# Wider moving operands in a two-layer transformer step: paired high and low activations for the first FFN matrix, token-major gate and branch projections, bias vectors loaded first

## The chip, the core and the metric

The program runs on one core of a Trainium2 chip. Its matrix engine (PE) multiplies a stationary 128x128 tile with a moving operand of up to 512 columns; the vector engine (DVE) and the scalar engine (ACT) work on rows of 128 partitions; SP issues the transfers. The metric is the device time of one execution in microseconds (us). What counts as computed is the whole of the reference: both token groups through both layers, and the two context states.

## The reference, cut to what matters

256 tokens (128 context and 128 latent) of width 2048 go through two layers. The layers' weights are float32 and each is used once per layer.

```python
shift1, scale1, gate1, shift2, scale2, gate2 = _modulation(cvec, p['w_mod'], p['b_mod'])
h = _rmsnorm(x, p['g_pre_mix']) * (1 + scale1) + shift1
au, av, q, k, v, ga, gb = jnp.split(h @ p['w_in'], SPLITS, axis=-1)
ya = _spatial_gating(au, av, ...)
yb, extra = attend(_heads(q), _heads(k), _heads(v))
merged = sigmoid(ga) * (ya @ p['w_pa']) + sigmoid(gb) * (_merge_heads(yb) @ p['w_pb'])
x = x + gate1 * _rmsnorm(merged @ p['w_out'], p['g_post_mix'])
h = _rmsnorm(x, p['g_pre_ffn']) * (1 + scale2) + shift2
f = jnp.square(jax.nn.relu(h @ p['w_ff1'])) @ p['w_ff2']
x = x + gate2 * _rmsnorm(f, p['g_post_ffn'])
```

## The kernel before, in words

**Products.** Every float32 factor is split into a high part (rounded to the float32r format) and a low part (the rest), and a product is the sum of three: high by high, low by high, high by low. A *job* is one weight tile of 128x1024 numbers: a transfer into `raw`, a high part `wh` that ACT writes, a low part `wl` that DVE writes (`split`, L319), and its matmuls (`mm_half`, L327). There are four buffers of `wh` and of `wl`, six of `raw`. A job covers two slices of 128 along the contracted dimension and 512 output columns. Eight jobs make a *group* for a contraction of 2048 (four for 1024), summed in one of two PSUM tiles `mm` of 128x1024.

**Two forms.** In the feature-major form (L346 to L352) the weight is stationary in 128x128 pieces and the activations of all 256 tokens move: 24 matmuls of 256 columns a job. In the token-major form (L339 to L344) the activations of 128 tokens are stationary and 512 weight columns move: 12 matmuls of 512 columns. Before, only the projections av and v are token-major, 64 of the 928 jobs.

**Stages.** The order is mixing, FFN, mixing, FFN. A mixing stage has 208 jobs: the input projections av, au, q, k, v (two groups each), four gate groups alternating with four branch projections pa, four alternating with pb, and four groups of wo. `post_pb` (L616) multiplies the gate in, adds the pa branch and splits the result; wo needs it feature-major. An FFN stage has 256 jobs in four blocks; in each, four groups of the first matrix (ff1) and four of the second (ff2). After an ff1 group `post_ff1` (L696) runs relu, square and the high part on ACT, then the low part on DVE.

**Around the stages.** At a boundary the columns are normed and the input of the next stage is made in four parts c = 0 to 3 by `h_part` (L286): DVE scales, DVE and ACT modulate, ACT rounds the high part, DVE takes the low part. `H_STEPS` lets parts 0 to 2 be issued ahead of the stage's first job and part 3 behind its third. The modulation matrices are read in 512 KB tiles throughout; 248 of them are dot products on DVE (`mod_dot`, two instructions of 128x1024 each), laid between the jobs by a quota and a load estimate. Sgu and attention run as background generators, one step per job (`pump`).

**What sets the order.** The program writes out one list of items by hand. Before each item `advance` issues loads, and splits while fewer than four split jobs wait for PE; then the item's matmuls follow, then dot products, then the group's post step. Each engine runs its own instructions strictly in that order.

## Time and profile before

| What | Value |
|---|---|
| median time of 3 runs | 2898.01 us (2897.16 to 2898.41) |
| profiled execution, first to last instruction | 2896.6 us |
| PE busy, weight loads busy | 98%, 94% |
| DVE busy, ACT busy | 71%, 46% |
| DMA, mean | 247 GB/s |
| feature-major matmuls (256 columns) | 20736 |
| token-major matmuls (512 columns) | 768 |

The profile gives no time of the profiled execution beyond its span, which is 1.4 us under the median. Busy time of PE is modelled from pipelined instructions that overlap each other, so the pace of matmuls is read from their starts, not from their mean durations. The groups view lists instructions by line, engine, operation and tile with busy time, mean duration and the idle time before them with what ended it; L80 is the helper through which all DVE and ACT instructions pass.

### The profile page before, as it was taken

To read this page: it belongs to the slowest core of one execution; us is meant where nothing else is said; L and a number is where in the kernel's file an instruction comes from. 1 tells how busy PE (TensorE), PEld (TensorE's weight loads), DVE (VectorE), ACT (ScalarE), POOL (GpSimd) and SP (SyncE) were. 2 spreads that over 40 slices of the span, in tenths; PEclk is the share of its full clock that TensorE was granted. 3 is DMA by queue.
4 is the path that set the end of the run, shared out by engine and by line. 5 is a ranking of instruction groups with operands and counts; after the bars stand their busy time and mean duration, and the time that the engine had idled before them with its cause. 6 is when DMAs were issued, how large, how long until landed. Compare 5 with 4: busy or idle time off the path is not lost.

```text
span 2896.6 us, 54382 instructions
## 1 busy us (share of the span) xinstructions
PE 2837.1 (98%) x22792; PEld 2718.1 (94%) x22792; DVE 2069.7 (71%) x2585; ACT 1331.0 (46%) x1614; POOL 0.7 (0%) x6
## 2 busy tenths in 40 slices
PE   7999999999999999999999999999999999999997
PEld 5788899998999999999979989999979999999997
DVE  4665778888688898888667887777566565665445
ACT  4344454444544534434454445544554444353443
POOL 0000000000000000000000000000000000000000
PEclk9999999999999999999999999999999999999999
DMA  8978877789568888888677786677666666666553
GB/s 346 383 257 309 284 234 234 264 283 347 191 226 275 273 274 269 282 272 275 239 278 245 225 285 220 206 239 246 248 239 201 209 213 219 215 204 190 181 184 109
DMA packets 199062, 714.91 MB, mean 247 GB/s; under 512 B 22304, under 2 KB 24864, under 8 KB 198816
## 3 DMA queue, kind: packets, MB, share of 16 engines
q1 hardware_dynamic: 198816, 711.43, 72.3%
q8 instruction: 178, 2.92, 0.4%
q14 instruction: 68, 0.56, 0.0%
HBM read 705.04 MB, written 6.31 MB: 246 GB/s over the span
## 4 chain that ended last, share of the span: by engine, by line
PE 95%; DVE 3%; ACT 1%; DMA 1%; issue 0%; SPq 0%; ACTq 0%; DVEq 0%
PE mm L350 29%; PE mm L351 28%; PE mm L352 28%; PE mm L342 2%; PE mm L343 2%; PE mm L344 2%; DVE u L80 2%; PE aux L237 2%; PE aux L256 1%; ACT u L80 1%; DMA u<-wm 0%; DVE wl L80 0%; DMA bmod<-bmod 0%; PE aux L497 0%; PE aux L539 0%
## 5 line engine op out<-in xcount | busy, mean ns | idle before, releaser
L350 PE MATMUL mm<-u,wh 128*128 128x256 f32 x6912 | 1962.3, 284 | 0.0
L351 PE MATMUL mm<-u,wh 128*128 128x256 f32 x6912 | 1956.7, 283 | 4.6 <-DVE u L80 4.6
L352 PE MATMUL mm<-u,wl 128*128 128x256 f32 x6912 | 1955.7, 283 | 0.0
L80 DVE TENSOR_TENSOR wl<-raw,wh 128x1024 fp32r<-128x1024 f32 x928 | 1122.6, 1223 | 575.1 <-ACT wh L80 564.9
L80 ACT ACTIVATE wh<-raw 128x1024 fp32r<-128x1024 f32 x928 | 972.9, 1058 | 1184.3 <-PE mm L351 1061.7
L350 PEld LDWEIGHTS mm<-u,wh 128*128 128x128 f32 x6912 | 1326.4, 192 | 20.4 <-issue 14.1
L351 PEld LDWEIGHTS mm<-u,wh 128*128 128x128 f32 x6912 | 1326.6, 192 | 6.0 <-DVE u L80 5.7
L352 PEld LDWEIGHTS mm<-u,wl 128*128 128x128 f32 x6912 | 1326.6, 192 | 0.0
L80 DVE SCALAR_TENSOR_TENSOR mraw<-mraw,sbc 128x1024 f32<-128x1024 f32 x225 | 275.7, 1225 | 7.8
L80 DVE SCALAR_TENSOR_TENSOR junk<-mraw,sbc 128x1024 bf16<-128x1024 f32 x225 | 274.3, 1219 | 0.0
L80 ACT ACTIVATE u<-u 128x1024 f32<-128x1024 f32 (+4 forms) x141 | 130.1, 926 | 112.8 <-DVE u L80 106.8
L80 DVE TENSOR_TENSOR u<-u,u 128x1024 fp32r<-128x1024 f32 (+4 forms) x98 | 100.8, 1028 | 97.3 <-ACT u L80 96.2
L80 ACT ACTIVATE u<-mm 128x1024 f32<-128x1024 f32 (+1 forms) x95 | 86.7, 925 | 156.0 <-PE mm L352 139.8
L80 DVE TENSOR_TENSOR u<-u,mm 128x1024 f32<-128x1024 f32 (+1 forms) x54 | 63.6, 1180 | 64.5 <-PE mm L352 52.7
L342 PE MATMUL mm<-wh,u 128*128 128x512 f32 x256 | 102.6, 401 | 4.4 <-ACT u L80 4.4
L343 PE MATMUL mm<-wh,u 128*128 128x512 f32 x256 | 101.3, 396 | 3.1 <-DVE u L80 3.1
L344 PE MATMUL mm<-wl,u 128*128 128x512 f32 x256 | 100.5, 393 | 0.0
L342 PEld LDWEIGHTS mm<-wh,u 128*128 128x128 f32 x256 | 48.6, 190 | 22.0 <-ACT wh L80 6.7
L343 PEld LDWEIGHTS mm<-wh,u 128*128 128x128 f32 x256 | 48.6, 190 | 14.8 <-DVE u L80 5.4
L344 PEld LDWEIGHTS mm<-wl,u 128*128 128x128 f32 x256 | 48.5, 189 | 10.3
L237 PE MATMUL aux<-mraw,csw 128*32 128x512 f32 (+1 forms) x336 | 44.5, 590 | 12.0 <-DMA mraw<-wm 11.9
L80 ACT ACTIVATE u<-u,mv 128x128 f32<-128x128 f32 x114 | 40.6, 431 | 17.8 <-DVE u L80 15.9
(91 smaller groups left out, 682.4 us busy)
## 6 DMA issues: line engine op xcount, KB each, us to landing
raw<-f SPq DMA_DIRECT2D x512, 512.0 KB, 4.4
mraw<-wm SPq DMA_DIRECT2D x301, 512.0 KB, 4.5
raw<-wi SPq DMA_DIRECT2D x288, 512.0 KB, 4.6
u<-wm SPq DMA_DIRECT2D x83, 512.0 KB, 9.1
raw<-wo SPq DMA_DIRECT2D x64, 512.0 KB, 4.6
raw<-pa SPq DMA_DIRECT2D x32, 512.0 KB, 4.5
raw<-pb SPq DMA_DIRECT2D x32, 512.0 KB, 4.7
u<-xT SPq DMA_DIRECT2D x8, 512.0 KB, 6.7
```

The lines of the kernel that those rows point to most:

```text
L80: return fn(out, *a, **k)
L237: nc.tensor.matmul(p[32 * c:32 * c + 32, :128 * nb], csw[:, kt, :], r[:, kt - k0, :], start=kt < 4, stop=kt > 11, skip_group_check=True, t ...
L256: nc.tensor.matmul(o[:, :T], ones, t[:, b, :], start=first and b == 0, stop=last and b == n - 1)
L342: nc.tensor.matmul(o, hh[:, s], wh[:, j, :], start=first, stop=False)
L343: nc.tensor.matmul(o, hl[:, s], wh[:, j, :], start=False, stop=False)
L344: nc.tensor.matmul(o, hh[:, s], wl[:, j, :], start=False, stop=last)
L350: nc.tensor.matmul(o, wh[:, j, s], hh, start=first and b % 2 == 0, stop=False, **kw)
L351: nc.tensor.matmul(o, wh[:, j, s], hl, start=False, stop=False, **kw)
L352: nc.tensor.matmul(o, wl[:, j, s], hh, start=False, stop=last, **kw)
```

## The change

**First FFN matrix.** ff1 in both layers, and au, q and k in layer 1, get a third form (`two`). The activations' high and low parts lie side by side in one tile (`pair`), so that a stationary piece of `wh` meets both in one matmul of 512 columns; the piece of `wl` meets the high part in one of 256. A job covers four contraction slices and 256 output columns (`_halves` lays the weights out so), a group is four jobs, and ends in two halves of 256 tokens that are summed at eviction: ACT copies the one, DVE adds the other, then the post step runs on 128x512.

**Token-major.** The eight gate groups and the pa and pb groups take the token-major form. Their elementwise work stays as it is; the merged result is token-major and is turned by eight PE transposes per pb group in a background generator `merge`, whose outputs wo waits for in the list (`merged`).

**Loads.** `bmod` and `gv` are loaded behind `cT`, no longer behind the first weight tiles. Parts 1 to 3 of `h_part` are made in two steps of two blocks instead of one of four.

```diff
+TWO = (1,)
+LAST = [11, 4, 11, 4]
...
+    nc.sync.dma_start(bmod, io["bmod"])
+    nc.sync.dma_start(gv, io["gv"])
...
-    def hi_lo(t, hi=None, lo=None):
-        hi = u4(F32R) if hi is None else hi
-        lo = u4(F32R) if lo is None else lo
-        act(hi, t, AF.Copy)
-        tt(lo, t, f(hi), op=OP.subtract)
-        return hi, lo
+    def pair():
+        return u4(F32R).rearrange("p (k h t) -> p k h t", k=2, h=2)
+
+    def hi_lo(t, hl):
+        act(hl[:, :, 0, :], t, AF.Copy)
+        tt(hl[:, :, 1, :], t, f(hl[:, :, 0, :]), op=OP.subtract)
...
-            t, hi, lo, s = todo.pop(0)
-            tt(lo[:, s, :], t[:, s, :], f(hi[:, s, :]), op=OP.subtract)
-
-        t, hi, lo = tiles
+            t, hl, s, u = todo.pop(0)
+            tt(hl[:, u, 1, :], t[:, s, :], f(hl[:, u, 0, :]), op=OP.subtract)
+
+        t, hls = tiles
...
-            act(hi[:, s, :], t[:, s, :], AF.Copy)
-            todo.append((t, hi, lo, s))
+            hl, u = hls[b0 // 2], slice(b0 % 2, b0 % 2 + n)
+            act(hl[:, u, 0, :], t[:, s, :], AF.Copy)
+            todo.append((t, hl, s, u))
...
-            t, hi, lo = v4(u4()), v4(u4(F32R)), v4(u4(F32R))
-            hs.append((hi, lo))
-            h_part(todo, (t, hi, lo), r2, l, ma, mb, c, ((0, 1), (1, 1), (2, 2)) if c == 0 else ((0, 4),), c in H_FLUSH)
+            t, hls = v4(u4()), [pair(), pair()]
+            hs.extend(hls)
+            h_part(todo, (t, hls), r2, l, ma, mb, c, ((0, 1), (1, 1), (2, 2)) if c == 0 else ((0, 2), (2, 2)),
+                   c in H_FLUSH)
...
+        if G.two:
+            wh, wl = (w.rearrange("p a b -> p (a b)").rearrange("p (k c) -> p k c", k=4) for w in (wh, wl))
+            for j in range(4):
+                kt = 4 * job.kh + j
+                hl = G.rhs[kt // 2][:, kt % 2]
+                for b in range(2):
+                    o = G.ps[:, 512 * b:512 * b + 512]
+                    s = slice(128 * b, 128 * b + 128)
+                    kw = dict(skip_group_check=True)
+                    nc.tensor.matmul(o, wh[:, j, s], hl.rearrange("p h t -> p (h t)"), start=kt == 0, stop=False, **kw)
+                    nc.tensor.matmul(o[:, :T], wl[:, j, s], hl[:, 0, :], start=False, stop=kt == 4 * G.n - 1, **kw)
+            return
+        n = (2 if job.kh < 2 else 4) if G.part else 2 * G.n
...
             if G.tok:
                 for g in range(2):
                     o = G.ps[:, 512 * g:512 * g + 512]
-                    s = slice(128 * g, 128 * g + 128)
-                    nc.tensor.matmul(o, hh[:, s], wh[:, j, :], start=first, stop=False)
-                    nc.tensor.matmul(o, hl[:, s], wh[:, j, :], start=False, stop=False)
-                    nc.tensor.matmul(o, hh[:, s], wl[:, j, :], start=False, stop=last)
+                    hh, lo = (hl[:, h, 128 * g:128 * g + 128] for h in range(2))
+                    nc.tensor.matmul(o, hh, wh[:, j, :], start=first, stop=False)
+                    nc.tensor.matmul(o, hh, wl[:, j, :], start=False, stop=False)
+                    nc.tensor.matmul(o, lo, wh[:, j, :], start=False, stop=last)
             else:
+                hh, lo = hl[:, 0, :], hl[:, 1, :]
                 for b in range(4):
                     o = G.ps[:, T * b:T * b + T]
                     s = slice(128 * b, 128 * b + 128)
                     kw = dict(skip_group_check=True)
                     nc.tensor.matmul(o, wh[:, j, s], hh, start=first and b % 2 == 0, stop=False, **kw)
-                    nc.tensor.matmul(o, wh[:, j, s], hl, start=False, stop=False, **kw)
+                    nc.tensor.matmul(o, wh[:, j, s], lo, start=False, stop=False, **kw)
                     nc.tensor.matmul(o, wl[:, j, s], hh, start=False, stop=last, **kw)
...
+    def ftiles(src, rhs, post, two):
+
+        if not two:
+            return gtiles(src, Group(8, rhs, lambda ps: post(v4(ps), 0)))
+
+        def half(b0):
+            def done(ps):
+                t = v4(s2(), 2)
+                p = ps.rearrange("p (b h t) -> p b h t", b=2, h=2)
+                act(t, p[:, :, 1, :], AF.Copy)
+                tt(t, t, p[:, :, 0, :], op=OP.add)
+                post(t, b0)
+            return done
+
+        return [j for h in range(2) for j in gtiles(src[4 * h:4 * h + 4], Group(4, rhs, half(2 * h), two=True))]
 
...
-                tt(t, t, m.pop(j), op=OP.add)
-                hi, lo = u4(F32R), u4(F32R)
-                act(hi, t, AF.Copy, scale=0.5)
-                dve.scalar_tensor_tensor(lo, t, 0.5, f(hi), op0=OP.mult, op1=OP.subtract)
-                mg.append((v4(hi), v4(lo)))
+                bg.append(merge(t, m.pop(j)))
             return post
+
+        def merge(t, ma):
+            tt(t, t, ma, op=OP.add)
+            yield
+            for e in range(2):
+                o = aux()
+                for b in range(2):
+                    for g in range(2):
+                        c = 512 * g + 256 * e + 128 * b
+                        nc.tensor.transpose(o[:, T * b + 128 * g:T * b + 128 * g + 128], t[:, c:c + 128], ident)
+                hl = pair()
+                act(hl[:, :, 0, :], v4(o, 2), AF.Copy, scale=0.5)
+                yield
+                dve.scalar_tensor_tensor(hl[:, :, 1, :], v4(o, 2), 0.5, f(hl[:, :, 0, :]), op0=OP.mult, op1=OP.subtract)
+                mg.append(hl)
+
+        def merged(n):
+            def go():
+                while len(mg) < n:
+                    pump(bg)
+            return go
 
...
         wi = io["wi"]
-        gi = lambda n, post, tok=False: gtiles(wi[l, n], Group(4, hs, post, tok))
+        gi = lambda n, post: gtiles(wi[l, n], Group(8, hs, post, True))
+        fi = lambda n, post: ftiles(wi[l, n], hs, post, l in TWO)
         for a in range(2):
-            seq.append(gi(2 + a, post_av(a), True))
+            seq.append(gi(2 + a, post_av(a)))
         for a in range(2):
-            seq.append(gi(a, post_au(a)))
+            seq.append(fi(a, post_au(a)))
...
-            seq.append(gtiles(io["pa"][l, j], Group(2, S["yav"], post_pa(j))))
+            seq.append(gtiles(io["pa"][l, j], Group(4, S["yav"], post_pa(j), True)))
...
-            seq.append(gtiles(io["pb"][l, j], Group(2, S["ybv"], post_pb(j))))
+            seq.append(gtiles(io["pb"][l, j], Group(4, S["ybv"], post_pb(j), True)))
         for o in range(4):
-            seq.append(gtiles(io["wo"][l, o], Group(4, mg, post_out(o))))
+            jobs = gtiles(io["wo"][l, o], Group(8, mg, post_out(o)))
+            if o == 0:
+                for k in range(4):
+                    seq += [merged(2 * k + 2), jobs[2 * k:2 * k + 2]]
+            else:
+                seq.append(jobs)
...
         def post_ff1(hid):
-            def post(ps):
-                t = u4()
-                act(t, ps, AF.Relu)
+            def post(t, b0):
+                act(t, t, AF.Relu)
                 act(t, t, AF.Square)
-                hi, lo = hi_lo(t)
-                hid.append((v4(hi), v4(lo)))
+                hid.append(pair())
+                hi_lo(t, hid[-1])
             return post
...
-                seq.append(gtiles(io["f1"][l, 4 * c + o], Group(4, hs, post_ff1(hid))))
+                seq.append(ftiles(io["f1"][l, 4 * c + o], hs, post_ff1(hid), True))
             for o in range(4):
-                seq.append(gtiles(io["f2"][l, o, 8 * c:8 * c + 8], Group(4, hid, post_ff2(c, o))))
+                seq.append(gtiles(io["f2"][l, o, 8 * c:8 * c + 8], Group(8, hid, post_ff2(c, o))))
...
-    items += [start_v, 4, start_norm, lambda: drain(bgm), 4, start_h(0, ((0, 1), (1, 1))), lambda: scale_x(1, 2, 3)]
+    items += [4, start_norm, lambda: drain(bgm), 4, start_h(0, ((0, 1), (1, 1))), lambda: scale_x(1, 2, 3)]
...
+def _halves(w):
+
+    t = _tiles(w, 512, 256)
+    return t.reshape(t.shape[:-4] + (t.shape[-4] // 2, 8, 128, 1024))
...
+    fine = _halves(I["w_in"])
+    for n in (0, 1, 4, 5, 6, 7):
+        for l in TWO:
+            A["wi"][l, n] = fine[l, n]
...
-    A["f1"] = _tiles(I["w_ff1"])
+    A["f1"] = _halves(I["w_ff1"])
```

The built order shows three places. In them `wl<-raw,wh` is the low part of one job's weights, a pair `junk` and `mraw` is one dot product, `s` and `u` with a number are working tiles, `mm` and `aux` are PSUM tiles, `mv` is the modulation.

DVE in an ff1 group of the second block of layer 0, before:

```order
L80 SCALAR_TENSOR_TENSOR mraw,tiny<-mraw,sbc 128x1024
L80 TENSOR_TENSOR u_10323<-u_10319,u_10322 128x1024
L80 TENSOR_TENSOR wl<-raw,wh 128x1024 x2
L80 SCALAR_TENSOR_TENSOR junk,tiny<-mraw,sbc 128x1024
L80 SCALAR_TENSOR_TENSOR mraw,tiny<-mraw,sbc 128x1024
```

and now, with one of its two halves from post step to post step:

```order
L84 TENSOR_TENSOR s_8788<-s_8788,mm 128x512
L84 TENSOR_TENSOR u_8793<-s_8788,u_8793 128x2x256
L84 TENSOR_TENSOR wl<-raw,wh 128x1024 x2
L84 SCALAR_TENSOR_TENSOR junk,tiny<-mraw,sbc 128x1024
L84 SCALAR_TENSOR_TENSOR mraw,tiny<-mraw,sbc 128x1024
L84 TENSOR_TENSOR wl<-raw,wh 128x1024 x2
L84 SCALAR_TENSOR_TENSOR junk,tiny<-mraw,sbc 128x1024
L84 SCALAR_TENSOR_TENSOR mraw,tiny<-mraw,sbc 128x1024
L84 TENSOR_TENSOR s_8891<-s_8891,mm 128x512
L84 TENSOR_TENSOR u_8896<-s_8891,u_8896 128x2x256
```

One DVE instruction per group of eight jobs became two per half of four, and the second of the two needs three ACT instructions that need the first. In the FFN of layer 0 blocks 1 to 3, the 24 halves hold 45 dot products between them; there were 48 in the 12 groups before.

DVE at the first FFN boundary, between the last of part 2 and part 3 (`u_7830` before, `u_6712` now), before:

```order
L80 TENSOR_TENSOR u_7718<-u_7716,u_7717 128x1024
L80 TENSOR_TENSOR wl<-raw,wh 128x1024 x4
L80 TENSOR_TENSOR u_7830<-u_6691,aux 128x1024
L80 TENSOR_SCALAR u_7830<-u_7830,mv 128x128 x4
L80 TENSOR_TENSOR u_7832<-u_7830,u_7831 128x1024
```

and now:

```order
L84 TENSOR_TENSOR u_6621<-u_6619,u_6621 128x2x256
L84 TENSOR_TENSOR wl<-raw,wh 128x1024 x4
L84 TENSOR_TENSOR u_6712<-u_5591,aux 128x512
L84 TENSOR_SCALAR u_6712<-u_6712,mv 128x128 x2
L84 TENSOR_TENSOR u_6712<-u_5591,aux 128x512
L84 TENSOR_SCALAR u_6712<-u_6712,mv 128x128 x2
L84 TENSOR_TENSOR u_6713<-u_6712,u_6713 128x2x256
L84 TENSOR_TENSOR u_6714<-u_6712,u_6714 128x2x256
```

Part 3 stands behind the same four splits as before. Before, the seventh job was the first to read it; now the fourth is.

PE behind a pb group of layer 0: the first row below is the last of the 12 matmuls of the first job of the next gate group, and the transposes of the merged tile `u_4445` stand behind that one job.

```order
L363 MATMUL mm<-wh,u_251 128x512
L673 MATMUL aux<-ident,u_4445 128x128 x4
L361 MATMUL mm<-wh,u_252 128x512
L362 MATMUL mm<-wl,u_252 128x512
L363 MATMUL mm<-wh,u_252 128x512
```

DVE, the work that makes `u_4445`:

```order
L84 SCALAR_TENSOR_TENSOR u_4445<-u_4445,mm 128x1024
L84 TENSOR_TENSOR wl<-raw,wh 128x1024
L84 TENSOR_TENSOR u_4445<-u_4445,u_3193 128x1024
L84 TENSOR_TENSOR wl<-raw,wh 128x1024 x2
L84 SCALAR_TENSOR_TENSOR u_4565<-aux,u_4565 128x2x256
```

Before, no PE instruction read this tile until wo; now the transposes do, and the sum with the pa branch stands one split behind the product.

More of the change, by code (lines that the diff above doesn't have):

```diff
@@ L411, in sgu @@
             bs = v4(S["bs"], 8)
-            S["ya"] = [(u4(F32R), u4(F32R)), (u4(F32R), u4(F32R))]
+            ya = [pair() for _ in range(4)]
             for k in range(4):
@@ L488, in attention @@
         def attention():
-            yb = [(u4(F32R), u4(F32R)) for _ in range(2)]
+            yb = [pair() for _ in range(4)]
             for t in range(4):
@@ L840, in body @@
     hs = [[] for _ in range(2 * DEPTH)]
-    def start_v():
-        nc.sync.dma_start(bmod, io["bmod"])
-        nc.sync.dma_start(gv, io["gv"])
     def start_rest():
@@ L876, in go @@
             if steps[0][0] == 0:
-                start["t"] = X[c], v4(u4(F32R)), v4(u4(F32R))
-                hs[0].append(start["t"][1:])
+                start["t"] = X[c], [pair(), pair()]
+                hs[0].extend(start["t"][1])
             if P["cap"] == 0:
```

106 lines of the change are left out of this document (55 added, 51 removed).

## The prediction

> **What bounds the kernel now.** I read the page first, then the waits of PE alone, then PE's timeline for the pace of its matmuls, then DVE and ACT in the stages that the change touches. The page's first part:
>
> ```profile
> PE 2837.1 (98%) x22792; PEld 2718.1 (94%) x22792; DVE 2069.7 (71%) x2585; ACT 1331.0 (46%) x1614; POOL 0.7 (0%) x6
> ```
>
> PE waits for next to nothing. Of its waits, these are all of those in front of the weight matmuls, in total, count and longest:
>
> ```profile
> PE mm L351 <- DVE u L80: 4.6, 4, 1.2
> PE mm L342 <- ACT u L80: 4.4, 1, 4.4
> PE mm L343 <- DVE u L80: 3.1, 4, 1.4
> ```
>
> Nine waits, 12.1 us, all for activations at the start of the program and at stage boundaries. No weight matmul waited for `wl`, the last product of the split. So PE's own instructions set the time, and the split buffers hide the rest. How full DVE is while PE never waits shows one window of the FFN of layer 0 (PE, weight loads, DVE, ACT in order):
>
> ```profile
> 900.00:1000.00 100.00, 100.00 (x836) 100.00 (x835) 86.24 (x114) 46.81 (x45) 0.00 (x0) 1.00 0.81 271
> ```
>
> DVE is busy 86% there. Its room is small, and that is where I look for the price.
>
> **The pace of PE.** Two stretches without a wait:
>
> ```profile
> 899.76 0.28 PE L351 MATMUL mm<-u,wh 128*128 128x256 f32 x1
> 902.88 0.28 PE L350 MATMUL mm<-u,wh 128*128 128x256 f32 x1
> 1515.07 0.39 PE L342 MATMUL mm<-wh,u 128*128 128x512 f32 x1
> 1524.59 0.39 PE L342 MATMUL mm<-wh,u 128*128 128x512 f32 x1
> ```
>
> From the first to the second row lie 26 matmuls of 256 columns: 3.12/26 = 0.1200 us. From the third to the fourth lie 42 of 512 columns: 9.52/42 = 0.2267 us. A wide matmul in place of two narrow ones saves 0.0133 us. The change has 5504 wide weight matmuls in place of 768, and 11264 narrow in place of 20736, so 4736 pairs became one: **-63.1 us**. Of these 2304 pairs are in the token-major groups, whose pattern is the one measured. The other 2432 are in the new form, where a wide and a narrow matmul alternate, which no row shows. I take 0.2267 + 0.1200 = 0.3467 for such a pair of instructions; the ends are 0.3600 (nothing saved, +32 us) and 0.3333 (another 32 us saved). The two pure paces fit a column rate plus the same fixed part, so the sum is nearest.
>
> A sentence apart: the Trainium skill, "TensorE: Matmul & The Clock Gate", section "Back-to-back issue gap", gives a warm gap of N/2.4 + 2.5 ns for a single matmul, by which a wide matmul would save 2.5 ns and not 13.3; as an estimate 4736 of them are -11.8 us, and the time would be 2962 us. The rows above measure the fixed part at five times that, so the sum goes by the rows.
>
> **Transposes.** 64 are added, all on PE's path. Four take
>
> ```profile
> 338.09 0.44 PE aux L526 x4
> ```
>
> so 64 x 0.11 = **+7.0 us**.
>
> **The wait of the transposes.** They stand one job behind the pb group. In the order before, the gate group ended where ACT starts its eviction, and four jobs later (4 x 2.88 = 11.52, at 542.13) DVE started on the branch:
>
> ```profile
> 530.61 1.02 ACT L80 ACTIVATE u<-mm 128x1024 f32<-128x1024 f32 x1 [1.94 <-PE mm L352]
> 542.13 1.22 DVE L80 SCALAR_TENSOR_TENSOR u<-u,mm 128x1024 f32<-128x1024 f32 x1
> 543.39 1.22 DVE L80 TENSOR_TENSOR u<-u,u 128x1024 f32<-128x1024 f32 x1
> ```
>
> DVE started at once. Now one split (1.14, below) lies between the product and the sum, so the sum ends 1.26 + 1.14 + 1.22 = 3.6 us behind the end of pb. PE needs 12 x 0.2267 = 2.72 for the job in front of the transposes, and begins it 0.16 before the last matmul's end (0.39 - 0.23): it waits 1.05 us if DVE is on time. With less time per job DVE will be later than in this row; I take 1.5, eight times: **+12 us**. The ends are 1.05 (8) and 3.5, a whole dot product in front (28).
>
> **The eviction of ff1.** Two turns of an ff1 group before, DVE and then ACT:
>
> ```profile
> 944.12 1.22 DVE L80 TENSOR_TENSOR u<-u,u 128x1024 fp32r<-128x1024 f32 x1 [1.51 <-ACT u L80]
> 945.26 2.35 DVE L80 TENSOR_TENSOR wl<-raw,wh 128x1024 fp32r<-128x1024 f32 x2
> 947.53 1.22 DVE L80 SCALAR_TENSOR_TENSOR junk<-mraw,sbc 128x1024 bf16<-128x1024 f32 x1
> 949.95 2.36 DVE L80 TENSOR_TENSOR wl<-raw,wh 128x1024 fp32r<-128x1024 f32 x2
> 967.16 1.23 DVE L80 TENSOR_TENSOR u<-u,u 128x1024 fp32r<-128x1024 f32 x1 [1.51 <-ACT u L80]
> ```
>
> ```profile
> 963.92 1.02 ACT L80 ACTIVATE u<-mm 128x1024 f32<-128x1024 f32 x1 [1.94 <-PE mm L352]
> 964.98 2.15 ACT L80 ACTIVATE u<-u 128x1024 f32<-128x1024 f32 x2
> 967.03 1.99 ACT L80 ACTIVATE wh<-raw 128x1024 fp32r<-128x1024 f32 x2
> ```
>
> A split costs DVE 2.27/2 = 1.135 us, a dot product 2.42. The low part waits for relu, square and high part, three ACT instructions in a row; DVE meets this once per group, idles 1.51 and still has its work done in the 23.04 us of eight jobs. The new form's pieces, by their nearest rows of 128x512:
>
> ```profile
> L80 ACT ACTIVATE u<-mm 128x512 f32<-128x512 f32 x22 | 12.0, 596 | 21.7 <-PE mm L344 12.1 <-PE mm L352 9.6
> L80 DVE TENSOR_TENSOR u<-u,mm 128x512 f32<-128x512 f32 x4 | 2.6, 684 | 10.0 <-PE mm L352 10.0
> L80 ACT ACTIVATE u<-u 128x512 f32<-128x512 f32 x16 | 9.7, 628 | 26.2 <-DVE u L80 26.2
> L80 DVE TENSOR_TENSOR u<-u,u 128x512 fp32r<-128x512 f32 x7 | 4.8, 690 | 3.0 <-ACT u L80 3.0
> ```
>
> For each half DVE adds (0.68), then has nothing to do until relu, square and high part are through (3 x 0.63 plus three handoffs, 2.0), and then the next split's `wh` stands behind them on ACT: its low part starts another 1.06 later, while the activations' low part (0.69) runs beside it. This wait cannot be hidden by being late, since the ACT chain now starts from DVE. Behind the waiting low part stand all further splits, and PE waits for those. Per half: 4 x 1.135 + 2 x 2.42 + 0.68 + 2.0 + 1.06 = 13.1 us, and 12.8 with the 45 dot products that 24 halves of blocks 1 to 3 hold in layer 0. PE needs 4 x 8 x 0.3467 = 11.09. DVE loses 1.7 a half, 13.7 in the eight halves of a block. The buffers give cover: three more split jobs (8.3) against 0.60 + 0.68 + 2.0 + 1.06 + 1.14 = 5.5 until the next is ready, 2.8 us. In ff2 DVE needs 8 x 1.135 + 4 x 2.42 + 1.2 = 20.0 of 23.04 and recovers. So PE waits 13.7 - 2.8 = 10.9 per block, three blocks: **+32 us**. With 0.5 us a half less or more it is 20 or 44. Block 0 and layer 1 hold half as many dot products or fewer: 12.8 less 2.4 is under 11.09, nothing.
>
> **The first ff1 group of a stage.** A job now reads four slices, so a part of the normed input lasts one job and not two. DVE and ACT before:
>
> ```profile
> 740.71 4.62 DVE L80 TENSOR_TENSOR wl<-raw,wh 128x1024 fp32r<-128x1024 f32 x4
> 745.25 1.21 DVE L80 TENSOR_TENSOR u<-u,aux 128x1024 f32<-128x1024 f32 x1
> 749.28 1.23 DVE L80 TENSOR_TENSOR u<-u,u 128x1024 fp32r<-128x1024 f32 x1 [1.66 <-ACT u L80]
> ```
>
> ```profile
> 739.44 3.89 ACT L80 ACTIVATE wh<-raw 128x1024 fp32r<-128x1024 f32 x4
> 756.56 1.02 ACT L80 ACTIVATE u<-mm 128x1024 f32<-128x1024 f32 x1 [1.94 <-PE mm L352]
> ```
>
> Part 3 was ready at 750.5, just as its first reader began (756.56 less two jobs of 2.88 is 750.8): it cost nothing. Now the fourth job reads it. By the same rows the third job ends near 743.6; the split in front of part 3 that needs the third job's buffer ends near 747.1; two scalings, four modulations and a low part of half the width (2.6 + 0.6) make its first half ready near 750.3. The group then ends at 750.3 + 2.77 + 11.09 = 764.2, against 756.5: 7.7 later, and 0.85 had been counted as saved. That is 8.6 twice, **+17 us** (ends 6.8, if the splits do not move, and 10.5). PE stands still for 6.7 us, and after standing still it is slow:
>
> ```profile
> 28.61 0.79 PE L342 MATMUL mm<-wh,u 128*128 128x512 f32 x1 [4.39 <-ACT u L80]
> 30.00:31.00 1.00, 1.00 (x4) 0.72 (x3) 0.94 (x1) 0.97 (x2) 0.00 (x0) 0.50 1.06 422
> 32.85 0.39 PE mm L342
> ```
>
> After 4.39 us of idle the granted clock (the third number from the end in the window's row) is 0.50, and the nine wide matmuls from 28.61 to 32.85 took 4.24 us where 9 x 0.2267 = 2.04 is the pace. 2.2 twice: **+4 us**, at least 0.
>
> **Mixing stages.** With token-major groups eight jobs take 21.8 us, not 23.04. DVE in a gate window:
>
> ```profile
> 500.00:600.00 100.00, 100.00 (x835) 100.00 (x835) 87.37 (x109) 40.61 (x40) 0.00 (x0) 1.00 0.77 259
> ```
>
> 0.874 x 23.04 = 20.1 us of work leaves 1.7 for its waits, and au, q, k in layer 1 add twelve instructions of 0.68. I take **+4 us** (0 to 15).
>
> **The start.**
>
> ```profile
> 1.65 1.85 SPq L139 DMA_DIRECT2D u<-xT  x4
> 16.48 0.33 SPq L842 DMA_DIRECT2D bmod<-bmod  x1
> 23.77 0.44 PE L219 MATMUL aux<-ident,s 128*128 128x128 f32 x2 [0.51 <-ACT s L80]
> 25.81 0.16 DVE L80 TENSOR_TENSOR mv<-mv,bmod 128x4 f32<-128x4 f32 x1 [5.49 <-DMA bmod<-bmod]
> ```
>
> The modulation waits 5.49 us for `bmod`. Without that, the shift's transposes at 23.77 come last and PE starts at most 1.7 us earlier; the two loads now hold up four activation loads by two issues (0.46 each, 1.85/4). **-0.5 us** (-1.7 to +1).
>
> **Sum.** -63.1 + 7.0 + 12 + 32 + 17.2 + 4.4 + 4 - 0.5 = +13.0. On the profiled span of 2896.6 that is 2909.6; the median lies 1.4 above the span, so **2911 us**.
>
> **Rivals.** *The eviction fits.* DVE absorbs the ACT chain as it does now: the +32 goes, 2879 us. For it: 14% of DVE's time is idle in the window; against: each half forces 3 us on it. Chance 0.17. *Half of it fits*, because some idle before was of use: 2895 us, no change, 0.12. *DVE becomes the bound in the mixing stages too*, from the point where its waits exceed 1.7 us in eight jobs: +15 in place of +4, with merges waiting 2.5 us (+8), 2930 us, 0.10. *The alternating pair saves nothing*: +32, 2943 us; it decides if weight loads, 94% busy, cannot run ahead of a narrow matmul; 0.04, with the skill's gap counted in.
>
> **How the numbers follow.** The forecast has 0.57. Its own terms' ends, taken as independent (root of the squared distances), lie 14 us below and 23 above it: 2897 to 2934. No change is within 0.2%, 5.8 us, about what a measurement of this kernel can tell. Faster: 0.17. Same: 0.12 and the forecast's low end, 0.04, so 0.16. Slower: 0.57 + 0.10 + 0.04, less that 0.04: 0.67. The range reaches to the first rival and over the third: 2880 to 2934.
>
> **What would show it.** In the profile after: wide starts 0.2267 apart and pairs 0.3467; PE waiting for `wl`, above 20 us in all, in the ff1 groups of blocks 1 to 3 of layer 0 and not in layer 1; a PE gap of 6 to 7 us in the first ff1 group of both layers; 64 transposes, with eight waits of 1 to 2.5 us on DVE; and low parts of `u` on DVE that idle about 2 us each for ACT. If PE's waits for `wl` stay under 10 us, the prediction is wrong and the kernel is faster.

## The result and the profile after

The change takes **2933.32 us** (median of 4 runs, 2931.12 to 2936.82) against 2898.21 for the kernel before beside it: ratio 1.0124, 95% interval 1.0109 to 1.0138. It is slower, as forecast, and inside the range, but by 35 us where 13 were forecast. The profiled execution has a span of 2935.0 us and its own time is 2936.82, so the span is 38.4 us longer than that of before.

The first part of the page of the change:

```profile
PE 2822.9 (96%) x18120; PEld 2479.3 (84%) x18120; DVE 2121.0 (72%) x2723; ACT 1387.4 (47%) x1815; POOL 0.7 (0%) x6
```

PE has 4672 instructions fewer and less work, and yet a longer span. Where the time went shows best by stage. Each stage boundary opens with the matmuls of the sum of squares with a tile of ones. First before, then after (PE's timeline; start, duration):

```profile
706.79 0.61 PE L740 MATMUL aux<-ones,s 128*128 128x2 f32 x4 [2.42 <-DVE s L80]
1473.91 0.61 PE L740 MATMUL aux<-ones,s 128*128 128x2 f32 x4 [2.16 <-DVE s L80]
2119.16 0.61 PE L740 MATMUL aux<-ones,s 128*128 128x2 f32 x4 [1.40 <-DVE s L80]
2881.46 0.61 PE L740 MATMUL aux<-ones,s 128*128 128x2 f32 x4 [3.15 <-DVE s L80]
```

```profile
704.79 0.61 PE L804 MATMUL aux<-ones,s 128*128 128x2 f32 x4 [2.42 <-DVE s L84]
1500.70 0.70 PE L804 MATMUL aux<-ones,s 128*128 128x2 f32 x3 [2.16 <-DVE s L84]
2152.32 0.61 PE L804 MATMUL aux<-ones,s 128*128 128x2 f32 x4 [1.41 <-DVE s L84]
2919.67 0.50 PE L804 MATMUL aux<-ones,s 128*128 128x2 f32 x3 [3.15 <-DVE s L84]
```

The differences of these starts, with the terms of the prediction divided by stage (the pace by its pairs: 1152 in each mixing stage, 384 more in that of layer 1, 1024 in each FFN stage):

| stage (with the boundary in front) | before | after | measured | forecast |
|---|---|---|---|---|
| mixing, layer 0 | 706.8 | 704.8 | -2.0 | -4.3 |
| FFN, layer 0 | 767.1 | 795.9 | +28.8 | +29.2 |
| mixing, layer 1 | 645.3 | 651.6 | +6.3 | -9.0 |
| FFN, layer 1 | 762.3 | 767.4 | +5.1 | -2.9 |
| end | 15.1 | 15.3 | +0.2 | 0 |

One such length is good to about 2 us: in five later kernels that run the same mixing stage of layer 0 it took 703.1 to 707.6. So layer 0 went as forecast, and the miss is layer 1: 15 us in its mixing stage, 8 in its FFN.

**The FFN of layer 0.** All waits of PE in the change, by what they waited for (total, count, longest), the rows that bear on the terms:

```profile
PE mm L349 <- DVE u L84: 17.4, 12, 5.9
PE aux L673 <- DVE u L84: 12.7, 8, 2.8
...
PE mm L350 <- DVE wl L84: 10.5, 15, 0.8
...
PE mm L349 <- ACT wh L84: 6.8, 12, 1.3
PE aux L455 <- DVE u L84: 5.3, 1, 5.3
...
PE mm L372 <- DVE wl L84: 3.0, 4, 0.8
```

PE now waits for the split's two products, `wh` and `wl`, in ff1 (L349, L350) and in the ff2 groups behind it (L372): 20.3 us in these three rows, none before. Behind one pair of these short waits the granted clock fell as well (two rows of PE's timeline, then the window in which they lie and the next one):

```profile
1218.42 0.38 PE L370 MATMUL mm<-u,wh 128*128 128x256 f32 x1 [0.75 <-ACT wh L84]
1219.68 0.39 PE L372 MATMUL mm<-u,wl 128*128 128x256 f32 x1 [0.76 <-DVE wl L84]
1217.54:1220.95 3.41, 1.90 (x14) 1.57 (x13) 3.16 (x4) 3.41 (x4) 0.00 (x0) 1.00 0.27 80
1220.95:1224.36 3.41, 3.41 (x18) 3.41 (x17) 3.38 (x6) 1.07 (x2) 0.00 (x0) 0.50 0.90 292
```

The same happened at 1016.15, behind waits of 1.26 and 0.77 us. The two falls cost about 3 us.

One half of ff1 in block 1 of layer 0, on DVE and on ACT:

```profile
957.63 0.68 DVE L84 TENSOR_TENSOR s<-s,mm 128x512 f32<-128x512 f32 x1
960.33 0.69 DVE L84 TENSOR_TENSOR u<-s,u 128x512 fp32r<-128x512 f32 x1 [2.03 <-ACT u L84]
961.29 2.36 DVE L84 TENSOR_TENSOR wl<-raw,wh 128x1024 fp32r<-128x1024 f32 x2 [0.26 <-ACT wh L84]
...
970.66 0.68 DVE L84 TENSOR_TENSOR s<-s,mm 128x512 f32<-128x512 f32 x1
```

```profile
958.34 1.30 ACT L84 ACTIVATE s<-s 128x512 f32<-128x512 f32 x2 [2.94 <-DVE s L84]
...
971.37 0.63 ACT L84 ACTIVATE s<-s 128x512 f32<-128x512 f32 x1 [4.87 <-DVE s L84]
```

From add to add DVE takes 970.66 - 957.63 = 13.03 us, of which 2.03 it stands behind relu, square and high part. ACT in its turn stands 2.94 and, in the next half, 4.87 us for DVE's add. Each engine waits for the other once per half.

**The first ff1 group.** PE's timeline, and a window of PE, weight loads, DVE and ACT with the granted clock third from the end:

```profile
745.44 0.79 PE L349 MATMUL mm<-u,wh 128*128 128x512 f32 x1 [5.93 <-DVE u L84]
750.36 0.39 PE L349 MATMUL mm<-u,wh 128*128 128x512 f32 x1
747.00:749.00 2.00, 2.00 (x8) 1.71 (x7) 0.00 (x0) 0.00 (x0) 0.00 (x0) 0.50 0.00 0
```

Part 3 of the normed input is 5.93 us late (5.94 in layer 1), and the eight pairs behind the gap take 4.92 us in place of 8 x 0.3467 = 2.77, at a clock of 0.50.

**The pair has two paces.** Two stretches of ff1 without any wait, the first in layer 0, the second in layer 1:

```profile
823.86 0.39 PE L349 MATMUL mm<-u,wh 128*128 128x512 f32 x1
827.67 0.39 PE L349 MATMUL mm<-u,wh 128*128 128x512 f32 x1
...
2208.06 0.40 PE L349 MATMUL mm<-u,wh 128*128 128x512 f32 x1
2219.36 0.40 PE L349 MATMUL mm<-u,wh 128*128 128x512 f32 x1
```

11 pairs in 3.81 us are 0.3464 each; 32 pairs in 11.30 are 0.3531. The granted clock is 1.00 in both. In layer 1 the 255 intervals of a whole block are of one kind: in blocks 1 and 3 intervals of 0.349, 0.350 and 0.361 follow each other in turn, 0.3533 in the mean, and in block 2 all but two are 0.346 or 0.347. Over all pairs, without those at a wait or a low clock (2340 are left), the mean is 0.3512.

**The mixing stage of layer 1.** The gating unit's matmuls run in the background between the jobs. PE, then DVE, then ACT, around their one long wait:

```profile
1658.04 1.65 PE L455 MATMUL aux<-u,u 128*128 128x128 f32 x6 [5.32 <-DVE u L84]
```

```profile
1656.77 1.22 DVE L84 TENSOR_TENSOR u<-u,u 128x1024 f32<-128x1024 f32 x1
1657.90 0.68 DVE L84 TENSOR_TENSOR s<-s,mm 128x512 f32<-128x512 f32 x1
1660.23 1.23 DVE L84 TENSOR_TENSOR wl<-raw,wh 128x1024 fp32r<-128x1024 f32 x1 [1.65 <-ACT wh L84]
```

```profile
1652.93 0.57 ACT L84 ACTIVATE s<-mm 128x512 f32<-128x512 f32 x1
1658.61 0.63 ACT L84 ACTIVATE u<-s 128x512 f32<-128x512 f32 x1 [5.11 <-DVE s L84]
```

The scaling at 1656.77 that these matmuls read is late on DVE, which has been busy without a gap since 1648.36; the add behind it keeps ACT waiting 5.11 us, and the next split's `wh` stands behind ACT's gelu, so that DVE idles 1.65. It is the mutual wait of ff1 again, in the au groups. And in the stage's first group, which the change leaves token-major as it was:

```profile
1533.60 0.50 PE L361 MATMUL mm<-wh,u 128*128 128x512 f32 x1 [2.50 <-ACT wh L84]
1534.86 0.71 PE L362 MATMUL mm<-wl,u 128*128 128x512 f32 x1 [0.76 <-DVE wl L84]
1536.00:1538.00 2.00, 2.00 (x6) 1.51 (x6) 2.00 (x2) 0.39 (x1) 0.00 (x0) 0.50 0.80 289
```

Before, PE stopped here twice, 1.22 and 1.40 us, for parts of the normed input:

```profile
1497.23 0.49 PE L343 MATMUL mm<-wh,u 128*128 128x512 f32 x1 [1.22 <-DVE u L80]
1501.66 0.50 PE L343 MATMUL mm<-wh,u 128*128 128x512 f32 x1 [1.40 <-DVE u L80]
```

Now there is one long stop for a split, and the clock halves behind it.

### The profile page after: what moved, and what is told of

It is laid out like the page before. It is cut to its first block, busy times and chain, and to the rows that moved or that the text cites. A ratio compares the mean times of both kernels' runs of the same rounds, so it can differ in the third digit from the quotient of the medians.

```text
span 2935.0 us, 45382 instructions
## 1 busy us (share of the span) xinstructions
PE 2822.9 (96%) x18120; PEld 2479.3 (84%) x18120; DVE 2121.0 (72%) x2723; ACT 1387.4 (47%) x1815; POOL 0.7 (0%) x6
## 4 chain that ended last, share of the span: by engine, by line
PE 79%; DVE 12%; issue 4%; ACT 4%; DMA 1%; SPq 0%; DVEq 0%; ACTq 0%
PE mm L349 13%; PE mm L370 12%; PE mm L372 11%; PE mm L371 11%; PE mm L361 7%; PE mm L362 7%; PE mm L363 7%; PE mm L350 7%; DVE wl L84 5%; DVE u L84 3%; DVE junk L84 2%; PE aux L243 2%; ACT wh L84 2%; DMA mraw<-wm 1%; DVE mraw L84 1%
## 5 line engine op out<-in xcount | busy, mean ns | idle before, releaser
L349 PE MATMUL mm<-u,wh 128*128 128x512 f32 x2432 | 866.3, 400 | 24.4 <-DVE u L84 17.4
L370 PE MATMUL mm<-u,wh 128*128 128x256 f32 x2944 | 837.6, 285 | 2.0 <-ACT wh L84 2.0
L372 PE MATMUL mm<-u,wl 128*128 128x256 f32 x2944 | 834.7, 284 | 3.0 <-DVE wl L84 3.0
L371 PE MATMUL mm<-u,wh 128*128 128x256 f32 x2944 | 834.3, 283 | 0.0
L350 PE MATMUL mm<-u,wl 128*128 128x256 f32 x2432 | 686.8, 282 | 10.5 <-DVE wl L84 10.5
L370 PEld LDWEIGHTS mm<-u,wh 128*128 128x128 f32 x2944 | 564.6, 192 | 17.5 <-issue 11.7
L349 PEld LDWEIGHTS mm<-u,wh 128*128 128x128 f32 x2432 | 459.8, 189 | 141.1 <-DVE u L84 22.0
L372 PEld LDWEIGHTS mm<-u,wl 128*128 128x128 f32 x2944 | 564.4, 192 | 3.8 <-DVE wl L84 3.8
L371 PEld LDWEIGHTS mm<-u,wh 128*128 128x128 f32 x2944 | 564.6, 192 | 0.1
L350 PEld LDWEIGHTS mm<-u,wl 128*128 128x128 f32 x2432 | 462.8, 190 | 15.3 <-DVE wl L84 15.2
L361 PE MATMUL mm<-wh,u 128*128 128x512 f32 x1024 | 407.5, 398 | 5.3 <-ACT u L84 2.7
L362 PE MATMUL mm<-wl,u 128*128 128x512 f32 x1024 | 400.9, 392 | 1.5 <-DVE wl L84 1.5
L363 PE MATMUL mm<-wh,u 128*128 128x512 f32 x1024 | 400.9, 392 | 0.2 <-DVE u L84 0.2
L361 PEld LDWEIGHTS mm<-wh,u 128*128 128x128 f32 x1024 | 193.3, 189 | 58.0 <-issue 11.9
L363 PEld LDWEIGHTS mm<-wh,u 128*128 128x128 f32 x1024 | 193.2, 189 | 42.0 <-DVE u L84 0.9
L362 PEld LDWEIGHTS mm<-wl,u 128*128 128x128 f32 x1024 | 193.4, 189 | 40.3 <-DVE wl L84 2.1
L84 ACT ACTIVATE s<-s 128x512 f32<-128x512 f32 x128 | 80.9, 632 | 152.1 <-DVE s L84 150.1
```

The source lines that it names most:

```text
L84: return fn(out, *a, **k)
L349: nc.tensor.matmul(o, wh[:, j, s], hl.rearrange("p h t -> p (h t)"), start=kt == 0, stop=False, **kw)
L350: nc.tensor.matmul(o[:, :T], wl[:, j, s], hl[:, 0, :], start=False, stop=kt == 4 * G.n - 1, **kw)
L361: nc.tensor.matmul(o, hh, wh[:, j, :], start=first, stop=False)
L362: nc.tensor.matmul(o, hh, wl[:, j, :], start=False, stop=False)
L363: nc.tensor.matmul(o, lo, wh[:, j, :], start=False, stop=last)
```

## The experiments

The theory after the trace of the change: each half of ff1, and of au, q, k in layer 1, costs a mutual wait of DVE and ACT; the merge and the late part 3 cost their waits; the pair's slow pace makes up the rest. The rivals: DVE's work as such is too much, or the token-major groups are to blame in layer 1. All times are medians; differences "against the change" are to 2933.32, measured beside the same kernel before (2897.2 to 2898.2 in every comparison). An interval is 4 us wide to each side, so a difference under some 6 us between two kernels is read from their stages and traces, not from the medians alone. Lengths of stages by the same starts as above, one profiled execution each, are in this table:

| kernel | median | ratio to before (95%) | mixing 0 | FFN 0 | mixing 1 | FFN 1 |
|---|---|---|---|---|---|---|
| the change | 2933.3 | 1.0109 to 1.0138 | 704.8 | 795.9 | 651.6 | 767.4 |
| token-major part alone | 2898.5 | 0.9998 to 1.0017 | 703.4 | 767.5 | 646.0 | 764.2 |
| half groups alone | 2939.1 | 1.0130 to 1.0160 | 705.1 | 797.3 | 655.2 | 764.0 |
| ff1's chain put off | 2900.7 | 1.0006 to 1.0025 | 707.6 | 765.9 | 651.8 | 761.4 |
| part 3 first | 2927.4 | 1.0091 to 1.0125 | 703.1 | 792.8 | 650.6 | 761.5 |
| wide, then narrow | 2928.2 | 1.0091 to 1.0121 | 703.3 | 791.4 | 653.0 | 762.8 |
| no halves in mixing | 2931.5 | 1.0100 to 1.0130 | 703.5 | 795.8 | 648.1 | 766.6 |
| gating unit later | 2936.8 | 1.0119 to 1.0149 | 704.6 | 805.2 | 647.9 | 764.2 |
| merge later | 2919.5 | 1.0060 to 1.0094 | 695.5 | 794.6 | 643.9 | 763.9 |
| token-major, merge later | 2885.1 | 0.9943 to 0.9972 | 695.5 | 768.8 | 639.5 | 762.9 |
| all waits taken out | 2870.5 | 0.9894 to 0.9923 | 698.0 | 761.7 | 639.9 | 756.7 |

### The two parts apart

Token-major alone: ff1 and layer 1's au, q, k go back to three narrow matmuls.

```diff
-TWO = (1,)
+TWO = ()
-                seq.append(ftiles(io["f1"][l, 4 * c + o], hs, post_ff1(hid), True))
+                seq.append(ftiles(io["f1"][l, 4 * c + o], hs, post_ff1(hid), False))
```

> The change with only its token-major part: ff1 and layer 1's au, q, k are feature-major again, three narrow matmuls each, as before the change. If the parts add, the mixing stage of layer 0, which has nothing else in it and became 2.0 us shorter, gives -2, the mixing stage of layer 1 about the same or a little more, and the FFN stages nothing: -4 to -8 us, about 2892. By the prediction's own terms -30.7 + 7.0 + 12 + 4 - 0.5 = -8.2. If the token-major groups are what made layer 1's mixing stage 6.3 us longer, then -2 + 6 = +4, about 2902.

Half groups alone: gates, pa and pb feature-major, `post_pb` with the sum and the split of before.

```diff
-            seq.append(gi(10 + j, post_gate("sg")))
+            seq.append(gi(10 + j, post_gate("sg"), False))
-            seq.append(gtiles(io["pa"][l, j], Group(4, S["yav"], post_pa(j), True)))
+            seq.append(gtiles(io["pa"][l, j], Group(4, S["yav"], post_pa(j))))
```

> The change with only its half groups (ff1 in both layers, au, q, k in layer 1): the gates and branches are feature-major again and the 64 transposes are gone. By the prediction's terms -32.4 + 32 + 17.2 + 4.4 = +21, about 2919. By the trace of the change (FFN stages +28.8 and +5.1, and the part of layer 1's mixing stage that belongs to the halves) +35 to +42, about 2937.

The half groups alone give 2939.1, +41 to before: all of the loss, as the trace of the change had it and twice what the prediction's terms had. The token-major part alone gives 2898.5, no change: neither of the expectations. Its FFN stages and layer 1's mixing stage are within 2 us of before, and the 30.7 us of pace hardly show; the run with the merge later (below) says where they are. By the medians the two parts make 7 us more than the change, by the spans of the profiled executions (-0.3 and +40.3 against +38.4) 2 us more.

### ff1's chain put off

```diff
-                act(t, t, AF.Relu)
-                act(t, t, AF.Square)
-                hid.append(pair())
-                hi_lo(t, hid[-1])
+                p = pair()
+                hid.append(p)
+                def go():
+                    act(t, t, AF.Relu)
+                    act(t, t, AF.Square)
+                    act(p[:, :, 0, :], t, AF.Copy)
+                    yield
+                    tt(p[:, :, 1, :], t, f(p[:, :, 0, :]), op=OP.subtract)
+                latq.append(go())
...
+            pump(latq)
             pump(bgm)
```

> The change, with the chain behind the eviction of a half of ff1 put off: relu, square and high part are issued behind the next split on ACT, the low part a job later, so that DVE does not stand in front of them. Theory (the chain's wait on DVE is what costs the FFN of layer 0): PE's waits for wh and wl in blocks 1 to 3 there, 26 us by its timeline, go: -18 to -26 against the change, about 2910. Rival (DVE's work as such, with the add that is new, fills the half): -8 or less, 2925 or more.

2900.7: -32.6 against the change, more than the theory had. A half on DVE in this kernel, and PE's waits for splits in its ff1 groups:

```profile
960.29 0.68 DVE L84 TENSOR_TENSOR s<-s,mm 128x512 f32<-128x512 f32 x1
960.89 1.22 DVE L84 TENSOR_TENSOR wl<-raw,wh 128x1024 fp32r<-128x1024 f32 x1
963.95 1.23 DVE L84 TENSOR_TENSOR wl<-raw,wh 128x1024 fp32r<-128x1024 f32 x1 [1.84 <-ACT wh L84]
965.09 0.68 DVE L84 TENSOR_TENSOR u<-s,u 128x512 fp32r<-128x512 f32 x1
...
972.79 0.68 DVE L84 TENSOR_TENSOR s<-s,mm 128x512 f32<-128x512 f32 x1
```

```profile
PE mm L350 <- DVE wl L84: 0.8, 1, 0.8
PE mm L349 <- ACT wh L84: 0.2, 1, 0.2
```

DVE's busy time on the page is the same (2120.1 against 2121.0 us), and so is the number of its instructions. Only the wait moved: the low part at 965.09 no longer idles, and the half takes 12.50 in place of 13.03 us. That, and the one split that DVE has done ahead of it, is enough for PE not to wait: 17.3 us in these two rows became 1.0, and FFN 0 is as long as before the change. The rival, work as such, falls.

### Part 3 first

```diff
-H_STEPS = [3, 0, 0, 1]
+H_STEPS = [[], [4, 0, 0, 0], [3, 0, 0, 1], [4, 0, 0, 0]]
```

> The change, with part 3 of the normed input of both FFN stages issued before the first job and not behind the third. Theory (four splits stand in front of it on DVE): the gaps of 5.9 us in the first ff1 group of both layers fall to 1 us or less, the cold clock behind them goes too: -12 to -17 against the change, about 2918. Rival (the modulations and low parts of the normed input themselves end as late): under -5, 2929 or more.

-5.9: half of the theory, just above the rival. The gap for part 3 is gone and another stands in its place; PE's timeline and a window behind it:

```profile
740.37 0.50 PE L349 MATMUL mm<-u,wh 128*128 128x512 f32 x1 [2.57 <-ACT wh L84]
741.63 0.58 PE L350 MATMUL mm<-u,wl 128*128 128x256 f32 x1 [0.76 <-DVE wl L84]
743.00:745.00 2.00, 2.00 (x8) 1.63 (x7) 1.98 (x2) 0.16 (x1) 0.00 (x0) 0.50 0.82 301
```

The split for the fifth job now stands behind part 3 on ACT. PE waits 3.3 us in place of 5.9, and this is long enough for the clock to halve all the same; I had counted the clock as saved.

### Wide matmuls before narrow ones

```diff
-            for j in range(4):
-                kt = 4 * job.kh + j
+            for low in range(2):
+                for j in range(4):
+                    kt = 4 * job.kh + j
...
+                        if low:
+                            nc.tensor.matmul(o[:, :T], wl[:, j, s], hl[:, 0, :], start=False, stop=kt == 4 * G.n - 1, **kw)
+                        else:
+                            nc.tensor.matmul(o, wh[:, j, s], hl.rearrange("p h t -> p (h t)"), start=kt == 0, stop=False, **kw)
```

> The change, with the matmuls of a half's job in another order: the eight wide ones first, then the eight narrow ones, instead of wide and narrow in turn. The alternating pair is 0.3467 us apart in some stretches and 0.3533 in others, without a wait. Theory (the alternation itself makes the slow pace, and the runs are of pure pace then): every pair costs 0.3467, 11 to 12 us less in the 2432 pairs; `wl` is needed 1.8 us later in a job, which takes part of PE's waits for it. -11 to -18 against the change, about 2919. Rival (the pace has to do with the size of the tiles or the place in memory, not with the order): 0 to -4.

-5.1, between the two. The jobs in PE's timeline:

```profile
804.62 2.00 PE L353 MATMUL mm<-u,wh 128*128 128x512 f32 x8
...
807.41 1.78 PE L353 MATMUL mm<-u,wh 128*128 128x512 f32 x7
```

From 804.62 to 807.41 a job takes 2.79 us, against 8 x 0.3467 = 2.77 and 8 x 0.3533 = 2.83 for the alternating order. The slow pace is gone in this order, for 0.02 us a job. At the mean of 0.3512 a job took 2.81, so 304 jobs save 304 x 0.02 = 6 us; nothing is left over for the waits for `wl`, which came back as waits for `wh`. So the slow pace belongs to the alternating order, since the same tiles in the other order have one pace only; what makes one stretch of alternating pairs slow and the next fast was not found.

### No halves in mixing; the gating unit later

```diff
-TWO = (1,)
+TWO = ()
```

> The change, with au, q and k of layer 1 feature-major again, so that only ff1 has half groups. Theory (the halves' add on DVE keeps ACT waiting, and through it the splits and the background work on PE): the mixing stage of layer 1 becomes as long as in the kernel with token-major groups alone, 646.0 against 651.6: -5 to -7 against the change, about 2927, and the wait of the gating unit's matmuls (5.3 us) is gone, although 384 pairs of matmuls lose 5.1 us of pace. Rival (layer 1's mixing stage is long because of the token-major groups): +3 to +6.

```diff
+            yield
+            yield
             del S["lng"], S["lnb"]
```

> The change, with the gating unit's matmuls issued two jobs later behind the scaling of its input on DVE. Theory (they stand on PE in front of the weight matmuls, and wait for a DVE that is late): the wait of 5.3 us and what follows it, 7 us in all, is gone, and nothing else waits in its place: -5 to -7 against the change, about 2927. Rival (DVE is behind there in any case, and the next split is late next): 0 to -2.

Without the halves in au, q, k the stage is 3.5 us shorter and the 5.3 us wait is gone (0.37 us is left of it), although 384 pairs lose their pace; the median moves by 1.9, less than the theory had, and no more than the intervals leave open. With the matmuls two jobs later the wait is gone too and the stage 3.7 shorter, but part of it came back as PE waits for the next splits (0.87 and 0.77 at 1717, which the change did not have). The whole kernel did not become faster, 2936.8: the generator's two extra steps move where dot products are laid in layer 0 (54 before the marker of FFN 0 in place of 56), and two more now stand on DVE in the boundary in front of FFN 0, from 706.84 to 711.67, where PE has a wait that the change does not have:

```profile
712.28 0.69 PE L273 MATMUL aux<-ident,tiny 128*128 128x128 f32 x2 [6.11 <-DVE tiny L84]
```

So this run says something on its stage and nothing on the median.

### The merge later

```diff
             tt(t, t, ma, op=OP.add)
             yield
+            yield
```

> The change, with the merge's transposes issued one job later behind its sum on DVE. Theory: the eight waits in front of the transposes, 12.7 us, go, since a job of 2.7 us covers all of them but one: -10 to -13 against the change, about 2922. Rival (the low parts of the merged tiles then come late to the first wo group): -5 or less.

-13.8: the row `L673`, 12.7 us in eight waits, has no successor among PE's waits, and the two mixing stages are 9.3 and 7.7 us shorter. The same on the token-major part alone:

> The token-major part alone, with the merge's transposes a job later. Alone it measured 2898.5, no change. Theory (its gain of 30.7 us in pace was eaten by the merge's waits, by the transposes and by the parts of the normed input that are now made in halves): without the waits -11 to -14 against the token-major part alone, about 2886, which is faster than before the change. Rival (the gate window has no room on DVE): -6 or less, 2892 or more.

2885.1, 13.4 less than without and 12 under the kernel before (0.9943 to 0.9972). So the token-major form does pay, and one `yield` decides whether it shows. Of the 30.7 us of pace less 7.0 for the transposes, 12 arrive: 11.3 in layer 0's mixing stage, nearly all of its share, but only 5.8 in layer 1's, while the FFN stages are 2.3 longer. In layer 1's mixing stage some 3 of the missing 6 are in the two av groups at its start (47.8 us before from the first matmul to the next group, 50.6 here and 50.8 in the token-major part alone), behind the clock at 0.50, and 1.2 in the boundary in front.

### All waits taken out

The chain put off, part 3 first, wide before narrow, the merge later, no halves in mixing:

> The change with its waits taken out together: ff1's chain put off, part 3 of the normed input of the FFN stages first, wide matmuls before narrow ones, transposes a job later, au, q and k of layer 1 feature-major. If the costs measured one by one add: -32.6 - 5.9 - 5.1 - 13.8 - 1.9 = -59 against the change, 2874 us, 0.8% faster than before. If they overlap (the order and the put-off chain both take PE's waits for wl; a faster stage makes DVE late elsewhere): 2880 to 2890.

**2870.5 us**, ratio to before 0.9908 (0.9894 to 0.9923): the costs add, within 4 us. It beats both kernels. Its page and what PE still waits for in front of weight matmuls:

```profile
PE 2803.9 (98%) x18504; PEld 2497.8 (87%) x18504; DVE 2111.7 (74%) x2711; ACT 1379.6 (48%) x1795; POOL 0.7 (0%) x6
```

```profile
PE mm L353 <- DVE u L84: 6.7, 6, 1.4
...
PE mm L353 <- ACT wh L84: 4.8, 2, 2.4
```

No wait in the middle of a stage is left in these rows; all are in the first group of a stage. Two variants of this kernel:

```diff
-TWO = ()
+TWO = (1,)
```

> As the run with all waits taken out, but au, q and k of layer 1 with half groups, as in the change. If their add on DVE costs more than the pace brings there: 1 to 4 us longer than that run. If the wide matmuls in their own order bring the pace without the cost: 2 to 4 us shorter.

```diff
-H_STEPS = [[], [4, 0, 0, 0], [3, 0, 0, 1], [4, 0, 0, 0]]
+H_STEPS = [[], [3, 1, 0, 0], [3, 0, 0, 1], [3, 1, 0, 0]]
```

> As the run with all waits taken out, but part 3 of the normed input behind one split and not before the first job. With part 3 first, PE waited 2.57 + 0.76 us for the next split in each FFN stage in place of 5.9 for part 3. If the two can share: 2 to 5 us shorter in all; if part 3 is again what is late (one split of 1.1 us in front): within 2 us.

With halves in au, q, k 2877.0 (0.9915 to 0.9944), 6.5 longer, 5.9 of it in that stage: more than expected. Its trace has the wait of the gating unit's matmuls back, at 6.37 us against 0.37 without the halves, so what costs there is this wait and not the add as such. With the gating unit two jobs later the change's stage took 647.9, without halves 648.1: the halves pay for themselves there once the wait is gone. That both together would be the shortest was not tried on this kernel. With part 3 second 2872.9, within what can be told from the same; its wait is for part 3 again (3.56 us) and not for the split (2.42).

### The order of the three products

```diff
-                    nc.tensor.matmul(o, hh, wl[:, j, :], start=False, stop=False)
-                    nc.tensor.matmul(o, lo, wh[:, j, :], start=False, stop=last)
+                    nc.tensor.matmul(o, lo, wh[:, j, :], start=False, stop=False)
+                    nc.tensor.matmul(o, hh, wl[:, j, :], start=False, stop=last)
```

> The change, with the three products of a token-major slice in the order of the kernel before (high by high weights, low by high weights, high by low weights); the change has the low part of the activations last. Theory (with the low part last, PE no longer waits 1.2 and 1.4 us for parts of the normed input in the first group of layer 1's mixing stage, runs ahead, and meets one wait of 2.5 + 0.8 us for the next split, after which the granted clock is 0.50 for some 5 us): with the old order the two short waits are back, the long one is under 1 us, the clock stays at 1.00, and the group takes 48 us in place of 51: -2 to -4 us, about 2930. Rival (the parts of the normed input, made in halves now, keep ACT longer, and the split is late whatever PE does before): the wait for wh stays over 2 us and the clock drops, 0.

> The kernel with all waits taken out (2870.5) with the same order of the three products. By the theory of the long wait and the clock -2 to -4, about 2867; by the rival 0; and if the low weights are what is late in the other token-major groups, longer.

2932.2 and 2870.8: nothing, and the wait for `wh` is still there (2.31 and 2.30 us), with 0.20 us more per matmul behind it. (The 51 us of the expectation are those of the token-major part alone; in the change the two av groups took 49.7 us, with the old order 49.5.) My theory of the order falls. What is left is that the parts of the normed input are made in halves: their first half is ready early enough for PE not to stop for it, and PE then meets the split that stands behind all parts on ACT. That this is the cause was not shown by undoing it.

## Why the prediction was right in direction and wrong in size

**Right.** *The pace*: 0.2267 and 0.1200 hold in the token-major and in the remaining feature-major groups. *The merge's wait*: 12.7 us in eight waits, +12 forecast; the run with one more `yield` gave 13.8 back. *ff1's eviction*: 13.03 us for a half against 13.1, with the forced wait of 2.03 against 2.0; blocks 1 to 3 of layer 0 took 191.5, 192.9 and 196.2 us and, with the chain put off, 182.6, 182.6 and 184.2: 31 us, +32 forecast, some 7 of them in the ff2 groups, where I had expected DVE to recover, and about 3 by the two falls of the clock; the median gave 32.6 back. My sign for it, over 20 us in PE's waits for `wl`, did not come out by the letter: these are 13.5, and only 9.4 in the ff1 groups where I had placed it, because half of each wait is listed under `wh`, which is late one matmul earlier. *Part 3*: a gap of 5.9 us against 6.7, the first ff1 group ends 7.1 and 11.0 us later against the marker of its stage than before, 9.9 forecast with the clock; from the stage's own first weight matmul it is 8.5 and 9.4, and the rest is the boundary in front. *The clock behind it*: 2.15 us against 2.2. That the whole FFN of layer 0 came within 0.4 us is luck in part: the slow pairs cost it 3.5 us that I had not, and its first group and splits cost as much less.

**Mis-sized, and where the other 22 us went** (25 on the profiled executions). The waits that the prediction named are there; the step that failed is the size of three of its terms. The pace of the pairs, the +4 for the mixing stages and the nothing for layer 1's FFN were too small by 11, 8 and 2 us, and a slow clock at the start of layer 1's mixing stage was not in the sum at all, 4.7 us.

- *"I take 0.3467 for such a pair."* It measured 0.3467 or 0.3533, 0.3512 in the mean: 2432 x 0.0045 = 11 us that were not saved, 5 of them in layer 1's FFN and 2 in its mixing stage. In some stretches of an alternating stream the two pure paces add, in others not. I had named 32 us each way as the ends of this term and then left them out of the range.
- *"Mixing stages: +4."* The au, q, k halves of layer 1 have the same mutual wait as ff1, and in the au groups DVE also carries the gating unit, for which PE waits: 5.3 us of wait and some 1.5 behind it, in part at a low clock, about 1 more for splits. I had priced the eviction's chain in ff1 alone, and in mixing only its busy time; the run without these halves and its counterpart (+5.9) show the term, and the run with the gating unit later (-3.7 in the stage) that it hangs on that one wait.
- *"Nothing in block 0 and layer 1."* The last ff1 group of block 0 in layer 1 holds four dot products too, and its two halves took 13.03 us each on DVE (adds at 2255.85, 2268.88 and 2281.91) against PE's 11.3: some 2 us after DVE's lead, by estimate from PE's waits for splits there (0.35, 0.28 and 0.76 us).
- *Not in the sum at all*: the boundary in front of layer 1's mixing stage, 2.8 us longer (21.3 against 18.5 us from marker to first weight matmul), and its first group with one stop of 3.3 us and a clock of 0.50, 1.9 longer. I had priced the slow clock only where I saw a long gap coming. The boundary's 2.8 us are the clock's and not a cost of its instructions: behind the same wait of 2.16 us the clock was 0.50 in the change and stayed at 1.00 before, and the runs with part 3 first and with the gating unit later, with the same instructions there, had 1.00 and took 18.5 us. In all sixteen traces this boundary takes about 18.5, 19.8 or 21.3 us, with a mean granted clock of 1.00, 0.91 or 0.84. The change, behind the wait:

```profile
1500.84:1507.67 6.83, 6.82 (x30) 1.77 (x30) 3.68 (x4) 1.17 (x5) 0.00 (x0) 0.50 0.77 279
```

Of the rivals, "DVE becomes the bound in the mixing stages too" named the place (it had +11 there and +8 for the merges, 2930; the merges kept to the forecast's +12), and "the alternating pair saves nothing" named the pair, of whose 32 us 11 came. Each held in part; with the clock at the boundary they make most of the 22 us.

## What to carry to other kernels

When an eviction becomes ACT, then DVE, then ACT again, price the wait of each engine for the other as often as it happens, in every stage that gets the new form, and not their busy time: here 72% of DVE busy hid a loss of 33 us, and issuing the tail of the chain one job later gave it back without removing an instruction. A change that makes PE faster moves every producer's deadline forward: after such a change, shift the background steps and the parts of the next input by a job before judging it; here 35 us slower became 27 us faster, with the halves in mixing taken back and the wide matmuls laid before the narrow ones. Laying matmuls of one width together brought 5 us of that.
